# A retention decoder layer on one core: the up phase of its MLP as one written-out sequence of products

## The chip, the cores and the metric

The kernel runs on one NeuronCore of a Trainium2 chip. Five engines work side by side: TensorE (PE in the profile, its weight loads PEld) multiplies, VectorE (DVE) and GpSimd (POOL) do elementwise arithmetic, ScalarE (ACT) copies and applies functions, SyncE (SP) issues the DMAs. The metric is the device time of one execution in microseconds (us); the time of the kernel before is the median of 3 runs.

## The reference, cut to what matters

One decoder layer on 2048 positions of width 1024 in float32: a mixer of convolution and retention, cross-attention into 256 memory tokens, then a squared-ReLU MLP of hidden width 4096. After each part stands a LayerNorm of `alpha * x + f(x)`. The change touches the end of the cross-attention and the MLP.

```python
def memory_cross_attention(x, mem, w_xq, w_xk, w_xv, w_xo):
    ...
    p = jax.nn.softmax(s, axis=-1).astype(x.dtype)
    o = jnp.einsum('bhsm,bmhd->bshd', p, v).reshape(B, S, D)
    return o @ w_xo

def squared_relu_mlp(x, w_up, w_down):
    return jnp.square(jax.nn.relu(x @ w_up)) @ w_down

def reference(...):
        ...
        xa = memory_cross_attention(x, mem, w_xq[l], w_xk[l], w_xv[l], w_xo[l])
        x = layer_norm(DN_ALPHA * x + xa, ln2_g[l], ln2_b[l])
        ff = squared_relu_mlp(x, w_up[l], w_down[l])
        x = layer_norm(DN_ALPHA * x + ff, ln3_g[l], ln3_b[l])
```

## The kernel before

A float32 product is made of three passes: each operand is split into a high part (a copy by ScalarE in the type float32r, CAST in the profile) and a low part (operand minus high part), and `passes` (line 123) multiplies high by high, high by low and low by high. Both matrix products of the MLP are done as Winograd's form of Strassen's scheme: a 2 x 2 product of blocks takes seven products, numbered 1 to 7, of operands that are sums of blocks. Each product is four steps of three matmuls, 128 x 128 by 128 x 512.

**Up phase** (`up_phase`, line 958, called once for each half `h` of the positions, with 16 units `f` each). `up_weights` (886) loads the two raw tiles `ur` of the next unit, has GpSimd make four sums (`us`, `ur`, 128 x 512), and splits seven operands into tiles `uo`: copies on ScalarE, low parts on VectorE, for product 4 on GpSimd. `x_operand` (859) does the same for the position side (`er` loaded, `ehi` and `elo`), once for each half. The seven products run in the order 1, 2, 3 of the unit before, 6, 4 of the unit before, 7, 5. Products 1, 6, 5 and 3 add up in one accumulator `ua`; between them ScalarE takes a snapshot of it (`snapshot`, 943, tile `sn`), and the next product into `ua` has to wait for that. `squared` (930) adds a product and a snapshot on VectorE, applies ReLU and square on ScalarE, and stores the hidden block `hs` to DRAM. Beside this `down_weights` (898) prepares the operands of the down weights, 16 jobs spread over the phase: loads `dr`, four sums `ds` on GpSimd, seven copies and low parts `dw`, seven stores to `wdo_d`.

**Down phase** (`down_all`, line 1102, 32 steps `k`, again seven products each, at the places `u` = 0 to 6). `w_load` (1005) loads weight operands (`do`), four steps ahead, `h_load` (1016) hidden blocks (`hr`); `h_sum` (1028) makes their sums on VectorE and `h_split` (1040) the operands `ho`, with low parts on VectorE for products 6, 7 and 3 and on GpSimd for the others. `add_to` (1072) adds each product to the accumulators `acc` on VectorE. A `Norm` (1081) finishes a row of 128 positions: statistics on VectorE, the root on GpSimd, the scaling on ScalarE, gain and bias half on VectorE, half on GpSimd (`affine`, 180).

**End of cross-attention** (loop at line 1194). For each block of 128 positions scores (`psc`) and softmax, then the output product `po` (`d_out`, 786) with transposes hooked into it: `d_probs` (773, tile `dp`) of the probabilities, and `x2_turn` (806, tiles `xt`, `xv`, `xs`) of normalised rows, from which the position operands are stored to `xo_d`. The two transpose into the same few PSUM banks.

**What sets the order.** TensorE follows the program's order throughout these phases (`ordered["pe"]`). For VectorE, ScalarE and GpSimd a scheduler at compile time chooses the order, from priorities and modelled times, until `ordered["rest"]` is set, which happens in the last unit of the up phase (line 1244); after that they too follow the program. Each engine runs its instructions in the order chosen. Loads on SP keep their order among themselves. Tiles live in a fixed number of slots per tag (line 37). All instructions of PE, DVE, ACT and POOL go through the wrapper at line 60, so that the profile gives L61 for all of them and they are told apart by their tiles.

## Time and profile before

| | us |
|---|---|
| median of 3 runs (2649.84 to 2657.35) | 2650.61 |
| the profiled execution | 2645.74 |
| its span, from the first to the last instruction | 2644.0 |
| end of cross-attention, from the last scores to the first up product (1290.1 to 1324.2) | 34.1 |
| up phase (1324.2 to 1986.5) | 662.3 |
| down phase, first 50 us (1986.5 to 2036.5) | 50.0 |
| down phase, the rest, up to its last matmul (2036.5 to 2628.9) | 592.4 |
| after the last matmul | 15.1 |

All positions in the trace are us from the start of the span. An engine's busy time is the time in which one of its instructions runs; consecutive matmuls overlap, so that the distance between starts, not the duration of one, tells what a matmul costs. Idle time in front of an instruction is put down to what released it.

### The profile page before, as it was taken

Reading aid. Unit: us, or ns where it says so; the run is one execution under the profiler, and the core shown is the slowest. Engines: PE = TensorE matmul, PEld = TensorE weight load, DVE = VectorE, ACT = ScalarE, POOL = GpSimd, SP = SyncE. Lnnn points to the kernel's source line nnn. Section 1 sums busy time; section 2 is a strip of 40 time slices with the busy share of each in tenths; the row PEclk is TensorE's granted clock in tenths of the full one; section 3 lists DMA queues with packets and bytes.
Section 4 is the critical chain, followed back from the end, with each engine's and each line's share of the span. In section 5 each row is a group of like instructions: output and inputs, shape, how many; then the busy total and the mean of one; then the engine's idle time right before and its main releaser. Section 6 shows DMA issues by size and latency. Waiting matters only on the chain.

```text
span 2644.0 us, 33973 instructions
## 1 busy us (share of the span) xinstructions
PE 2546.8 (96%) x12248; PEld 2152.1 (81%) x12248; DVE 1704.2 (64%) x2675; ACT 928.7 (35%) x1667; POOL 1002.3 (38%) x908
## 2 busy tenths in 40 slices
PE   8999999998999999999889999999998999999997
PEld 7999999987889888888777877777776888778885
DVE  6888888888885644444565556555544555775557
ACT  3222322223233622222456656566552222222221
POOL 3222432215555311221255453455522322552235
PEclk9999999999999999999999999999999999999998
DMA  5222322223633502222476676677769776787774
GB/s 171 64 61 74 121 80 70 76 92 129 207 121 120 183 25 96 76 69 87 147 246 247 246 251 214 222 267 262 252 222 386 253 257 238 265 317 257 247 250 155
DMA packets 246632, 471.09 MB, mean 178 GB/s; under 512 B 19392, under 2 KB 136640, under 8 KB 246464
## 3 DMA queue, kind: packets, MB, share of 16 engines
q1 hardware_dynamic: 237104, 460.37, 50.1%
q10 hardware_dynamic: 9360, 8.56, 1.1%
q8 instruction: 96, 1.57, 0.2%
q14 instruction: 72, 0.59, 0.1%
HBM read 328.34 MB, written 140.51 MB: 177 GB/s over the span
## 4 chain that ended last, share of the span: by engine, by line
PE 78%; DVE 6%; DMA 5%; POOL 5%; ACT 3%; issue 2%; SPq 0%; POOLq 0%; ACTq 0%; DVEq 0%
PE po L61 12%; PE da L61 11%; PE ua L61 10%; PE pj L61 9%; PE pjh L61 8%; PE psc L61 7%; PE dc L61 5%; PE uc L61 4%; PE pc L61 3%; PE db L61 2%; PE ub L61 2%; DMA do<-wdo_d 2%; POOL us L61 1%; POOL ds L61 1%; PE psY L61 1%
## 5 line engine op out<-in xcount | busy, mean ns | idle before, releaser
L61 PE MATMUL da<-do,ho 128*128 128x512 f32 x1536 | 368.7, 396 | 19.2 <-DVE acc L61 12.9
L61 PE MATMUL ua<-ehi,uo 128*128 128x512 f32 x1024 | 337.7, 400 | 27.3 <-ACT sn L61 25.1
L61 PEld LDWEIGHTS da<-do,ho 128*128 128x128 f32 x1536 | 292.8, 191 | 85.1 <-DVE acc L61 14.8
L61 DVE SCALAR_TENSOR_TENSOR cacc<-u,convw,cacc 128x512 f32<-128x512 f32 x480 | 353.9, 749 | 6.8
L61 PEld LDWEIGHTS ua<-ehi,uo 128*128 128x128 f32 x1024 | 195.8, 191 | 77.3 <-ACT sn L61 30.4
L61 POOL TENSOR_TENSOR ho<-hr,ho 128x512 fp32r<-128x512 f32 x96 | 131.6, 1380 | 207.5 <-ACT ho L61 159.8
L61 PE MATMUL ua<-elo,uo 128*128 128x512 f32 x512 | 203.7, 398 | 0.0
L61 PE MATMUL pjh<-whi,xhi 128*128 128x384 f32 x512 | 186.6, 365 | 0.0
L61 POOL TENSOR_TENSOR wlo<-wraw,whi 128x384 fp32r<-128x384 f32 x128 | 127.7, 1024 | 142.2 <-ACT whi L61 129.9
L61 PE MATMUL dc<-do,ho 128*128 128x512 f32 x768 | 180.4, 390 | 1.0 <-DMA do<-wdo_d 1.0
L61 PE MATMUL pjh<-whi,xlo 128*128 128x384 f32 x512 | 172.6, 337 | 0.0
L61 PE MATMUL pjh<-wlo,xhi 128*128 128x384 f32 x512 | 172.6, 337 | 0.0
L61 PEld LDWEIGHTS dc<-do,ho 128*128 128x128 f32 x768 | 143.9, 188 | 32.3 <-DMA do<-wdo_d 2.6
L61 PE MATMUL uc<-ehi,uo 128*128 128x512 f32 x512 | 165.4, 393 | 2.5 <-DVE hs L61 2.5
L61 ACT CAST ho<-hr 128x512 fp32r<-128x512 f32 x128 | 77.3, 618 | 252.1 <-DMA hr<-h_d 90.0
L61 PE MATMUL pj<-xhi,whi 128*128 128x512 f32 x384 | 153.8, 400 | 8.0 <-ACT whi L61 6.7
L61 PE MATMUL pj<-xhi,wlo 128*128 128x512 f32 x384 | 150.5, 392 | 0.1
L61 PE MATMUL pj<-xlo,whi 128*128 128x512 f32 x384 | 150.3, 391 | 0.0
L61 ACT ACTIVATE hs<-hs 128x512 f32<-128x512 f32 x192 | 121.1, 631 | 51.7 <-DVE hs L61 49.0
L61 DVE TENSOR_TENSOR acc<-acc,da 128x512 f32<-128x512 f32 x104 | 70.8, 684 | 88.0 <-PE da L61 88.0
L61 DVE TENSOR_TENSOR uo<-us,uo 128x512 fp32r<-128x512 f32 x96 | 79.0, 832 | 61.0 <-ACT uo L61 61.0
L61 PEld LDWEIGHTS uc<-ehi,uo 128*128 128x128 f32 x512 | 96.6, 189 | 24.5 <-DVE hs L61 2.9
(212 smaller groups left out, 6037.2 us busy)
## 6 DMA issues: line engine op xcount, KB each, us to landing
do<-wdo_d SPq DMA_DIRECT2D x245, 512.0 KB, 6.4
wdo_d<-dw SPq DMA_DIRECT2D x112, 512.0 KB, 2.7
ur<-in_w_up_dram SPq DMA_DIRECT2D x64, 512.0 KB, 5.2
h_d<-hs SPq DMA_DIRECT2D x128, 256.0 KB, 3.4
hr<-h_d SPq DMA_DIRECT2D x104, 256.0 KB, 3.2
wraw<-in_w_in_dram SPq DMA_DIRECT2D x64, 384.0 KB, 3.1
dr<-in_w_down_dram SPq DMA_DIRECT2D x32, 512.0 KB, 3.8
er<-xo_d SPq DMA_DIRECT2D x28, 512.0 KB, 4.8
```

Source lines behind the costliest of these rows:

```text
L61: ins = fn(*args, **kw)
```

## The change

The two calls of `up_phase` become one function, `up_all`, over 32 units with seven steps `n` each. The products keep their sequence. A list `stream` of all weight operands is walked beside it: in each step `up_make` prepares the operand that is needed eight steps later (four and six steps in the first two units). The sums and all low parts are made by VectorE. `late` holds a low part back until the next operand is begun. ReLU and square of a block come one step after its addition. `ordered["rest"]` is set in the last block of the cross-attention, so that from there on all engines follow the program.

What happens at the borders is put down by step number (`put`): the position operands of the first half are split during the last two output products and the first steps, those of the second half in steps 106 to 118; the jobs for the down weights (`dw_load`, `dw_make`) begin about every 11.4 steps and take eight; the weight operands of the first down products are loaded from step 210 on, the first hidden block from step 215.

In the down phase all low parts of `h_split` move to VectorE; the hidden block of the next step is loaded at place 2 of a step and used from place 5 on; a norm's scaling, gain and bias become two VectorE operations of 128 x 1024 (`scalar_tensor_tensor`), and the norms get other places. The last two norms of the cross-attention use the same form. Several tiles get other tags.

Removed functions, which stand above, are left out of the diff here.

```diff
-        return layer_norm(xr, l2g, l2b, x2_d[tt * P:(tt + 1) * P, :])
+        if tt < NT - 2:
+            return layer_norm(xr, l2g, l2b, x2_d[tt * P:(tt + 1) * P, :])
...
+    waiting = []
+    def late(fn):
+        flush()
+        waiting.append(fn)
+    def flush():
+        while waiting:
+            waiting.pop(0)()
...
+    def x_split(h, i, k):
+        raw = raws.pop((h, i, k))
+        hi = sb(XTAG[i], [P, 2, 512], "ehi", F32R)
+        lo = sb(XTAG[i], [P, 2, 512], "elo", F32R)
+        act.copy(hi, raw)
+        late(lambda: lo_dve(lo, raw, hi))
+        xo.setdefault((h, i), []).append((hi, lo))
...
+    def up_load(g):
+        if g < UPS:
+            a0, a1 = sb("R", [P, D], "ur0"), sb("R", [P, D], "ur1")
+            eload(a0, a["w_up"][2 * (g % NF)])
+            eload(a1, a["w_up"][2 * (g % NF) + 1])
+            wraws[g] = [a0, a1, None]
...
+    def up_make(g, i):
+        if not 0 <= g < UPS:
+            return
+        w = wraws[g]
+        a0, a1 = w[:2]
+        if i == 6:
+            w[2] = sb("V", [P, D], "us")
+            dve.tensor_tensor(w[2][:, c0], a1[:, c0], a1[:, c1], op=ALU.add)
+            dve.tensor_tensor(w[2][:, c1], w[2][:, c0], a0[:, c0], op=ALU.subtract)
+        elif i == 7:
+            dve.tensor_tensor(a1[:, c0], a0[:, c0], a1[:, c0], op=ALU.subtract)
+        elif i == 5:
+            dve.tensor_tensor(a0[:, c1], a0[:, c1], w[2][:, c1], op=ALU.subtract)
+        src = {1: a0[:, c0], 2: a0[:, c1], 3: a0[:, c1], 4: a1[:, c1]}.get(i)
+        if src is None:
+            src = {5: w[2][:, c0], 6: w[2][:, c1], 7: a1[:, c0]}[i]
+        z = sb("B" if made[0] % 10 in (6, 7) else "Z", [P, 2, 512], "uo", F32R)
+        made[0] += 1
         act.copy(z[:, 0, :], src)
...
+        late(lambda: lo_dve(z[:, 1, :], src, z[:, 0, :]))
+        wup[g, i] = z
+        if i == 4:
+            up_load(g + 2)
...
+    def dw_load(j):
+        b0, b1 = sb("Ya", [P, D], "dr0"), sb("Ya", [P, D], "dr1")
+        eload(b0, a["w_down"][2 * j])
+        eload(b1, a["w_down"][2 * j + 1])
+        draws[j] = b0, b1, sb("W", [P, 512], "ds")
...
+    def dw_make(j, n):
+        b0, b1, t2 = draws[j]
+        i = (1, 5, 2, 6, 7, 4, 3)[n]
+        if i == 5:
+            dve.tensor_tensor(b0[:, c0], b0[:, c1], b0[:, c0], op=ALU.subtract)
+        elif i == 6:
+            dve.tensor_tensor(t2, b1[:, c1], b0[:, c0], op=ALU.subtract)
+        elif i == 7:
+            dve.tensor_tensor(b0[:, c1], b1[:, c1], b0[:, c1], op=ALU.subtract)
+        elif i == 4:
+            dve.tensor_tensor(b1[:, c0], b1[:, c0], t2, op=ALU.subtract)
...
+        z = sb(("Yb", "Yb", "V")[dn[0] % 3], [P, 2, 512], "dw", F32R)
+        dn[0] += 1
+        act.copy(z[:, 0, :], src)
+        def low():
+            lo_dve(z[:, 1, :], src, z[:, 0, :])
+            sp.dma_start(wdo_d[j][i - 1], z.bitcast(F32))
+        late(low)
...
+    def up_all(at, ahead):
+        order = [1, 2, 3, 4, 6, 7, 5]
+        stream = [(m // 7 - (order[m % 7] in (3, 4)), order[m % 7]) for m in range(7 * UPS + 7)]
+        nextop = [5]
...
+        def add(c, f, tb, ps, snap):
+            t, dst = h_tile(c, f, tb)
+            dve.tensor_tensor(t, quarters(ps), quarters(snap), op=ALU.add)
+            squares(t, dst)
...
+            if c:
+                if u == 0:
+                    c.a = pp("ua")
+                    up_product(c.a, c, 1, True)
+                    c.s1 = snapshot(c.a)
+                elif u == 1:
+                    b = pw("ub")
+                    up_product(b, c, 2, True)
+                    add(c, 0, 0, b, c.s1)
+                elif u == 3:
+                    up_product(c.a, c, 6, False)
+                    c.s2 = snapshot(c.a)
+                elif u == 5:
+                    c.c = psm("uc")
+                    up_product(c.c, c, 7, True)
+                elif u == 6:
+                    up_product(c.a, c, 5, False)
+                    c.s3 = snapshot(c.a)
+            if last:
+                if u == 0:
+                    add(last, 1, 1, last.c, last.s3)
+                elif u == 2:
+                    up_product(last.a, last, 3, False)
+                    t, dst = h_tile(last, 0, 1)
+                    act.activation(t, quarters(last.a), AF.Relu)
+                    def go(t=t, dst=dst, ps=quarters(last.a)):
+                        dve.scalar_tensor_tensor(t, ps, 0.0, t, op0=ALU.max, op1=ALU.mult)
+                        sp.dma_start(dst, t)
+                    tail.append(go)
+                elif u == 4:
+                    up_product(last.c, last, 4, False)
+                    add(last, 1, 0, last.c, last.s2)
+            for fn in before:
                 fn()
-            b = pw("ub")
-            up_product(b, c, 2, True)
-            end(2)
-            squared(c, 0, 0, b, s1)
-            if last:
-                up_rest3(last)
-            up_product(c.a, c, 6, False)
-            end(6)
-            c.s2 = snapshot(c.a)
-            if last:
-                up_rest4(last)
-            c.c = psm("uc")
-            up_product(c.c, c, 7, True)
-            end(7)
-            up_product(c.a, c, 5, False)
-            s3 = snapshot(c.a)
-            squared(c, 1, 1, c.c, s3)
-            end(5)
-            last = c
-        up_rest3(last)
-        nxt(3)
-        up_rest4(last)
-        nxt(4)
+            for fn in at.get(n, ()):
+                fn()
+            while nextop[0] < min(n + 1 + ahead(n), len(stream)):
+                up_make(*stream[nextop[0]])
+                nextop[0] += 1
...
-        tag = "X" if i in (1, 2, 6, 7) else "Ya" if i in (5, 3) or f % 4 < 2 else "V"
+        tag = "X" if i in (2, 6, 7, 5) else "Ya" if i in (3, 4) or f % 4 < 2 else "V"
...
-        (lo_dve if i in (6, 7, 3) else lo_pool)(z[:, 1], src, z[:, 0])
+        late(lambda: lo_dve(z[:, 1], src, z[:, 0]))
...
+            self.mv, self.rs = mean_rstd(self.z, D)
         def finish(self):
-            affine(self.z, l3g, l3b, self.dst)
-    NORMS = {13: [(0, 0, 3)], 14: [(0, 1, 0), (0, 2, 3)], 15: [(0, 3, 0)], 16: [(0, 4, 0), (0, 5, 3)],
-             17: [(0, 6, 0)], 18: [(0, 7, 0)],
-             29: [(1, 0, 3)], 30: [(1, 1, 0), (1, 2, 3)], 31: [(1, 3, 0), (1, 4, 3), (1, 5, 4)]}
+            z = self.z
+            dve.scalar_tensor_tensor(z, z, self.mv[:, 0:1], self.g, op0=ALU.subtract, op1=ALU.mult)
+            dve.scalar_tensor_tensor(z, z, self.rs, self.b, op0=ALU.mult, op1=ALU.add)
+            sp.dma_start(self.dst, z)
...
+    NORMS = {13: [(0, 0, 3)], 14: [(0, 1, 3)], 15: [(0, 2, 3)], 16: [(0, 3, 2)],
+             17: [(0, 4, 3)], 18: [(0, 5, 1), (0, 6, 3)], 19: [(0, 7, 2)],
+             29: [(1, 0, 3)], 30: [(1, 1, 1), (1, 2, 3)], 31: [(1, 3, 0), (1, 4, 2), (1, 5, 4)]}
...
+                todo[5].append(lambda nx=nx: (h_sum(nx, 0), h_split(nx, 1), h_sum(nx, 1), h_split(nx, 2)))
+                todo[6].append(lambda nx=nx: (h_sum(nx, 2), h_split(nx, 6), h_sum(nx, 3), h_split(nx, 7)))
+                carry.append((0, lambda nx=nx: (h_split(nx, 5), h_split(nx, 3))))
+                carry.append((1, lambda nx=nx: h_split(nx, 4)))
...
-                if u == 5 and k + 2 < DOWN:
-                    h_load(k + 2, ["Hb", "Hb", "Hb", "Ha", "Hc", "Hc", "Hc"])
+                        w_load(j, (u + 5) // 2)
+                if u == 2 and k and k + 1 < DOWN:
+                    h_load(k + 1, ["Hb", "Hb", "Hb", "Ha", "Hc", "Hc", "Hc"])
...
+            if tt == NT - 1:
+                ordered["rest"] = True
...
+                out_hooks = [(2, lambda: part(0, "R")), (5, lambda: part(1, "R")), (8, lambda: part(2, "Z")),
+                             (10, lambda: part(3, "Z")), (11, lambda: d_probs(tt, 0)),
+                             (13, lambda: d_probs(tt, 1)), (14, lambda: part(4, "V"))]
...
+            out_hooks = [(1, n14.stats), (2, lambda: part(5, "V")), (4, n14.finish), (6, lambda: up_make(0, 1)),
+                         (8, lambda: part(6, "Z")), (9, lambda: up_make(0, 2)), (11, lambda: part(7)),
+                         (13, lambda: up_make(0, 6))]
...
+    put(0, n15.stats, lambda: x2_turn(NT - 2, 0), lambda: part(8))
+    put(1, n15.finish, lambda: x2_turn(NT - 2, 1), lambda: part(9))
+    put(2, lambda: x_load(0, *parts[11], "V"), lambda: part(10))
+    put(3, lambda: up_load(1), lambda: x_load(0, *parts[12], "V"))
+    put(4, lambda: part(11), lambda: x_load(0, *parts[13], "Z"))
+    put(5, lambda: part(12))
+    put(6, lambda: part(13))
+    put(7, lambda: x2_turn(NT - 1, 0))
+    put(8, lambda: x2_turn(NT - 1, 1))
...
+    for start, end, jobs in ((14, 105, range(8)), (119, 203, range(8, 16))):
+        for m, j in enumerate(jobs):
+            n0 = start + (end - start) * m // 8
+            put(n0 - 3, lambda j=j: dw_load(j))
+            for q, o in enumerate((0, 1, 3, 4, 5, 6, 7)):
+                put(n0 + o, lambda j=j, q=q: dw_make(j, q))
+    b0 = 7 * (NF - 1)
+    for i, n in ((1, 0), (2, 1), (6, 3), (7, 5), (5, 6), (3, 9), (4, 11)):
+        for q, k in enumerate((0, 2)):
+            tag = {0: "V", 1: "Ya", 2: "Yb"}[(2 * TURN.index(i) + q) // 2 % 3]
+            put(b0 + max(n - 2, 0), lambda i=i, k=k, tag=tag: x_load(1, i, k, tag))
+            put(b0 + n + 1 + q, lambda i=i, k=k: x_split(1, i, k))
...
+    e0 = 7 * (UPS - 1)
+    put(e0 - 7, lambda: [w_load(f, 1) for f in range(DEEP)])
+    put(e0 - 2, first_hidden)
+    for n, i in ((0, 2), (1, 6), (3, 7), (5, 5)):
+        put(e0 + n, lambda i=i: [w_load(f, i) for f in range(DEEP)])
+    put(e0 + 2, sums)
+    put(e0 + 3, lambda: h_split(0, 1))
+    put(e0 + 4, lambda: h_split(0, 2), lambda: load_acc(0, 0))
+    put(e0 + 5, lambda: h_split(0, 6))
+    put(e0 + 6, lambda: h_split(0, 7))
+    put(e0 + 7, lambda: h_split(0, 5))
+    put(e0 + 9, lambda: h_split(0, 3))
+    put(e0 + 11, lambda: h_split(0, 4))
+    up_all(at, lambda n: 4 if n < 7 else 6 if n < 14 else 8)
```

## Rows read from the trace of the kernel before

**Rows 1.** The page, part 1: busy time, share of the span, instructions of TensorE.
```profile
PE 2546.8 (96%) x12248; PEld 2152.1 (81%) x12248; DVE 1704.2 (64%) x2675; ACT 928.7 (35%) x1667; POOL 1002.3 (38%) x908
```
**Rows 2.** Stages: start:end length, busy (instructions) of PE PEld DVE ACT POOL, clock, DMA share, GB/s.
```profile
1290.10:1324.20 34.10, 25.28 (x113) 20.57 (x112) 25.37 (x34) 16.67 (x22) 5.70 (x6) 0.85 0.71 225
1324.20:1986.50 662.30, 632.51 (x2706) 511.87 (x2705) 375.56 (x456) 387.07 (x675) 326.19 (x229) 0.99 0.70 244
1986.50:2036.50 50.00, 42.44 (x156) 31.42 (x156) 22.98 (x29) 10.57 (x18) 11.94 (x10) 0.90 1.02 397
2036.50:2628.90 592.40, 579.76 (x2535) 477.98 (x2533) 375.31 (x485) 134.06 (x217) 218.83 (x187) 0.99 0.72 255
2628.90:2644.00 15.10, 0.11 (x1) 0.00 (x0) 7.58 (x13) 1.89 (x2) 7.69 (x10) 0.60 0.27 104
```
**Rows 3.** Two stretches without a wait, TensorE alone: busy (instructions), clock, DMA.
```profile
1440.00:1560.00 120.00, 120.00 (x523) 1.00 0.66 233
2060.00:2260.00 200.00, 200.00 (x884) 1.00 0.72 251
```
**Rows 4.** TensorE's waits in four stages: in total, times, longest us.
```profile
PE dp L61 <- DVE xv L61: 8.8, 1, 8.8
...
PE ua L61 <- ACT sn L61: 25.1, 11, 4.2
PE uc L61 <- DVE hs L61: 2.5, 1, 2.5
PE ua L61 <- ACT uo L61: 2.1, 1, 2.1
...
PE da L61 <- DVE acc L61: 12.6, 5, 4.1
```
**Rows 5.** One stretch of low clock, TensorE alone: busy (instructions), clock, DMA.
```profile
1341.70:1345.10 3.40, 2.92 (x7) 0.50 0.78 277
```
**Rows 6.** Timeline from 1560 to 1567: start, us, instruction, [idle before <- releaser].
```profile
1560.38 1.74 POOL L61 TENSOR_TENSOR ds<-dr 128x512 f32<-128x512 f32 x1
...
1563.49 0.62 ACT L61 CAST dw<-ds 128x512 fp32r<-128x512 f32 x1 [4.08 <-POOL ds L61]
...
1565.75 0.58 ACT L61 COPY sn<-ua 128x512 f32<-128x512 f32 x1
1566.38 0.50 PE L61 MATMUL ua<-ehi,uo 128*128 128x512 f32 x1 [3.90 <-ACT sn L61]
```
**Rows 7.** Low parts on VectorE, by tile (ns min/median/max); by group (busy, mean).
```profile
L61 DVE TENSOR_TENSOR uo<-ur,uo x96: 675/685/1790, 1288.4 to 1955.9; 128x512 fp32r<-128x512 f32 x96
...
L61 DVE TENSOR_TENSOR elo<-er,ehi x28: 1208/1226/2320, 1294.5 to 1667.7; 128x1024 fp32r<-128x1024 f32 x28
...
L61 DVE TENSOR_TENSOR dw<-ds,dw 128x512 fp32r<-128x512 f32 x48 | 44.2, 921 | 42.6 <-ACT dw L61 41.2
```
**Rows 8.** Timeline of VectorE with GpSimd idle.
```profile
2105.13 0.69 DVE L61 TENSOR_TENSOR acc<-acc,dc 128x512 f32<-128x512 f32 x1 [2.03 <-PE dc L61]
2105.73 0.69 DVE L61 TENSOR_TENSOR hr<-hr 128x512 f32<-128x512 f32 x1
```
**Rows 9.** Timeline from 2284 to 2294, in the down phase.
```profile
2285.95 1.74 POOL L61 TENSOR_TENSOR ho<-hs,ho 128x512 fp32r<-128x512 f32 x1
2286.46 1.77 DVE L61 TENSOR_TENSOR hs<-hr,hs 128x512 f32<-128x512 f32 x1
...
2292.48 2.07 PE L61 MATMUL da<-do,ho 128*128 128x512 f32 x4 [4.15 <-DVE acc L61]
```
**Rows 10.** DMA issues from 1400, from 1960 and from 2040: count, KB, median us to landing.
```profile
ur<-in_w_up_dram SPq DMA_DIRECT2D x24, 512.0 KB, 5.2
...
do<-wdo_d SPq DMA_DIRECT2D x42, 512.0 KB, 8.6
...
hr<-h_d SPq DMA_DIRECT2D x36, 256.0 KB, 2.9
```
**Rows 11.** Timeline of the tail: VectorE's add of the last product.
```profile
2634.77 0.67 DVE L61 TENSOR_TENSOR acc<-acc,da 128x512 f32<-128x512 f32 x1
```

More of the change, by code (lines that the diff above doesn't have):

```diff
@@ L1170, in down_all @@
             last = c
-        for _, fn in carry:
-            fn()
         down_product(last, last.c, 4, False)
         add_to(last, 1, 0, last.c)
-        o = Norm(1, 7)
+        t0 = T + 7 * P
+        o = Norm(acc[1, 7], l3[0], l3[1], out[t0:t0 + P, :])
         o.stats()
@@ L1183, in down_all @@
         t0 = T + 6 * P
-        layer_norm_last(z, l3g, l3b, out[t0:t0 + P, :], half_stats(z, st, 1))
+        layer_norm_last(z, l3[0], l3[1], out[t0:t0 + P, :], half_stats(z, st, 1))
     for tt in range(3):
@@ L1213, in hybrid_layer, with part @@
             if tt == NT - 1:
-                up_weights(0)
-                for i in TURN[:4]:
-                    x_operand(0, i)
-                out_hooks = [(11, lambda: d_probs(tt, 0)), (13, lambda: d_probs(tt, 1))]
+                up_load(0)
+                parts = [(i, k) for i in TURN for k in (0, 2)]
+                for n in range(4):
+                    x_load(0, *parts[n], ETAG[n])
+                def part(n, more=None):
+                    x_split(0, *parts[n])
+                    if more:
+                        x_load(0, *parts[n + 4], more)
@@ L1232, in first_hidden @@
         for n in range(4):
             last_sum.append(h_sum(0, n))
-    def first_down(i):
-        if i == 7:
-            load_acc(0, 0)
-        for f in range(DEEP):
-            if i not in (3, 4):
-                w_load(f, i)
-        for j in {2: (1,), 6: (2, 6), 7: (7,), 5: (5,)}.get(i, ()):
-            h_split(0, j)
-        if i == 5:
-            ordered["rest"] = True
-    up_phase(1, {NF - 1: [first_hidden]}, first_down)
-    for i in (3, 4):
-        h_split(0, i)
+    e0 = 7 * (UPS - 1)
```

175 lines of the change are left out of this document (63 added, 112 removed).

## The prediction

> **What bounds the kernel now.** I read the totals first, then the stages, then what TensorE waited for in each, then one wait of each kind in the timeline. TensorE works through 96% of the span [rows 1], so only its lost time can be won. The table of stages [rows 2] splits the part that the change touches: the end of cross-attention (34.1 us), the up phase (662.3), the first 50 us of the down phase, the rest of it (592.4) and what follows the last product (15.1). What the work itself needs comes from two stretches without a wait [rows 3]: 120 us hold 521 up matmuls (523 less the two cut by the edges), 0.2303 us each, and 200 us hold 882 down matmuls, 0.2267 us each. The same shape is slower in the up phase; nothing in the trace says why, so both stay. A phase has 32 units x 7 products x 12 matmuls = 2688. Then:
>
> - end of cross-attention: 96 matmuls x 0.2267 + 16 transposes (0.6 us per four) = 24.2; lost 9.9
> - up: 2688 x 0.2303 + 16 transposes (2.4) = 621.4; lost 40.9
> - first 50 us of down: 154 x 0.2267 = 35.0; lost 15.0
> - rest of down: 2534 x 0.2267 = 574.4; lost 18.0
>
> The waits [rows 4] name most of it: one of 8.8 us in front of the transposes `dp`, 29.7 in the up phase (25.1 of them for the snapshot `sn` on ScalarE), 12.6 in the rest of down for `acc` on VectorE. [...]
>
> Why does ScalarE snapshot late, being busy 387 of 662 us [rows 2]? In the timeline [rows 6] it stands 4.08 us in front of `dw<-ds`, whose source GpSimd is still subtracting (1.74 us for one sum), and the snapshot is queued behind that and four more copies; TensorE waits 3.90. VectorE in the down phase shows the same [rows 9]: operands of later products at 1.77 us apiece stand in front of the add that frees `da`; TensorE waits 4.15.
>
> **The change, part by part.**
>
> 1. *Sums and low parts to VectorE.* In the up phase GpSimd issues 229 instructions [rows 2]; by the code 224 are the moved sums and low parts (4 + 1 per unit, 4 per down job). VectorE then has 456 + 224 = 680. What one costs: `uo` has minimum 675, median 685, maximum 1790 ns [rows 7]: two modes, and the slow one lies in the timeline beside a two-input GpSimd operation [rows 9]. With GpSimd idle I take the fast mode; back to back they start 0.60 us apart [rows 8]. 680 x 0.60 + 28 wide ones x 0.56 more = 424 us of some 630: 67%. In the eight steps of a down job it is (8 x 15/7 + 11) x 0.60 = 16.9 of 22.1 us. Nothing on the path. If the slow mode had another cause, a rival below has the price.
>
> 2. *The order.* The sequence of products is the same in both kernels (1, 2, old 3, 6, old 4, 7, 5); new is that ScalarE and VectorE get theirs by place. A snapshot now stands at the head of its step, and its accumulator is written again two products later: 24 x 0.2303 = 5.5 us of slack. Weights are made eight products (22 us) ahead, and the low part one make later than its copy, so VectorE never stands waiting for a copy just issued. Of the 40.9 us lost in up I leave 8.5: 1.0 where product 3 of the last unit directly follows product 5 on one accumulator, as now; 3 for the seam between the halves, where x operands add a 1024-wide copy and low part per step (bounds: 0, and 6.4 as now); 4.5 for the first unit, below. Gain 32.4.
>
> 3. *End of cross-attention and first unit.* The wait of 8.8 us ended with `xv` on VectorE: weight and x operand work stood in front of it. Now VectorE comes to `xv` before that, so the stage takes 24.2 us. Gain 9.9. But VectorE's list is long there. From 1303.4 (end of the last but one output product) I add: statistics 1.5, the norm's two new 1024-wide operations 2.4, four wide low parts at 1.16, five 512-wide ones, another norm's statistics 1.5, two sums: 14.2 us, to 1318. Then it waits for product 2 (end 1320.6) and does add 0.6, norm 2.4, two wide low parts, a sum and the low part of weight 7: done at 1327.2. Product 7 is due at 1323.9 and can run 0.45 us without it: 2.8 us of wait, and a clock stretch behind it, 1.7. The 1024-wide operation with a scalar is in no row; I take 1.2, near the free `elo` (1226 ns), the bounds being 1.2 and its maximum 2.32 [rows 7]: up to 4.5 us more. Below, 0.
>
> 4. *Start of down.* From the end of unit 31's first product to the fourth product of k = 1 lie 18 products, 49 us. In it must land 29 weight tiles, four accumulators, a hidden block and the last stores: about 20 MB. The row of that stretch moved 397 GB/s with all engines full [rows 2]: 50 us. Nearly even, so I keep 5 of the 15.0 us (bounds 0 and 15). Gain 10. [...]
>
> 5. *Rest of down.* The norms leave ScalarE and GpSimd, so VectorE's slow mode goes there too. What is late next: after product 7 VectorE does an add, two sums and the low part of the next operand 1: 0.2 + 3 x 0.60 + 0.69 = 2.7 us, wanted at 2.72 + 0.45 = 3.17. It just fits, at cost 0; with a norm's end in front it may not, and I leave 2 of the 18.0. At 0.92 apiece (the mean of `dw<-ds` [rows 7]) for the last three it would be 3.6, 0.5 late in each of 31 steps: 15 us, the upper bound. The hidden block is now loaded at place 2 for use at place 5, 8.2 us, against 2.9 to land [rows 10]. Gain 16.
>
> 6. *Tail.* VectorE's last add starts at 2634.77 [rows 11], behind a norm that went over GpSimd and ScalarE. Now, from 2626.1: 0.2 + add 0.6, statistics 1.5, half statistics 0.6, norm 2.4 after 0.3 for the root: 2631.7. Gain 3.
>
> Sum: 32.4 + 9.9 + 10 + 16 + 3 = 71.3 us. The profiled execution took 2645.74 us (span 2644.0), 4.9 under the median 2650.61; the gain is taken off the median: 2579, said as 2580.
>
> **The rivals.**
>
> *The seams keep their price.* First unit 9, seam of the halves 6.4, start of down 15, some of the norms: 30 us more, 2609. For it: my lists for these places are the least sure, and DMA is full there. Against: each wait there was for an engine out of order, and loads are pulled ahead by 7 steps. Chance 0.14.
>
> *VectorE stays slow without GpSimd,* 0.92 us each, the mean of `dw<-ds` [rows 7], instead of 0.60. A down job comes every 11.4 steps (31.4 us), with 35.4 operations: 32.6 us, 1.2 late for each of 16 jobs, 19 us less the slack of 5.5; with the 15 of point 5 that is 28 us more, 2608. Against: the two modes. Chance 0.10.
>
> *The order was no cause:* the same waits stand at other places, and 30 us of up stay: 2610. Against: rows 6 shows a queue in which the urgent copy stands last. Chance 0.05.
>
> *Slower: a load late at the head of a queue.* ScalarE's copy of the next unit's first weight waits for a load that is asked for only after a low part one step later; it is wanted 11 - 2.8 = 8.3 us after that. Lateness blocks the snapshots behind it, and TensorE loses what passes the 5.5 us of slack. So it begins to cost at a landing of 13.8 us and eats the gain at 13.8 + 71/31 = 16.1; at 17 us it gives 31 x 3.2 = 99 us, 2680. The median landing of `ur` is 5.2, and 8.6 with the DMA engines full [rows 10]. Chance 0.06, half of it near 16 us, where it ends within the measurement. [...]
>
> **How the numbers follow.** The forecast has 0.65, around 2580: 2565 if nothing of points 2 to 5 is left, 2555 if in addition the up matmuls ran at 0.2267. With the seams and the slow VectorE the range is 2563 to 2617; outside lie the late load and the far ends. Measurements of this kernel tell 0.3% (8 us) from no change: faster 0.94, same 0.03, slower 0.03.
>
> **What would show it.** TensorE's wait for `sn` gone, and the up phase 630 us long, beginning ten us earlier; VectorE's `uo` with a maximum near 700 ns, GpSimd nearly idle; one wait at product 7 of the first unit; waits for `acc` under 2 us in all; up matmuls still at 0.230 us. It is wrong if ScalarE waits for `ur` or `er` in many units, or if TensorE waits for `ho` once in each k.

## The result, and the profile after

The kernel after takes 2575.86 us (median of 4 runs, 2574.07 to 2578.04), against 2650.9 for the kernel before beside it: a ratio of 0.971, 95% interval 0.970 to 0.973. The forecast was 2580, with 2563 to 2617 as its range. The profiled execution took 2576.22 us, its span 2574.4.

The page, part 1, the line that answers to [rows 1]:

```profile
PE 2531.4 (98%) x12248; PEld 2144.9 (83%) x12248; DVE 1785.3 (69%) x3027; ACT 907.7 (35%) x1650; POOL 447.7 (17%) x505
```

The stages, as in [rows 2]: start:end length, then busy time (instructions) of PE, PEld, DVE, ACT and POOL, granted clock, DMA share, GB/s. They are again the end of cross-attention, the up phase, the first 50 us of the down phase, the rest of it, and what follows the last product:

```profile
1293.50:1317.20 23.70, 23.69 (x113) 19.38 (x112) 19.33 (x27) 12.40 (x18) 3.84 (x3) 1.00 0.93 316
1317.20:1942.20 625.00, 621.40 (x2706) 507.71 (x2706) 448.97 (x693) 391.45 (x683) 2.04 (x3) 1.00 0.76 262
1942.20:1992.20 50.00, 45.57 (x187) 35.34 (x186) 24.88 (x40) 9.34 (x16) 0.00 (x0) 0.97 1.02 393
1992.20:2562.80 570.60, 569.86 (x2505) 469.14 (x2503) 389.58 (x603) 117.44 (x203) 10.79 (x30) 1.00 0.75 262
2562.80:2574.40 11.60, 0.20 (x1) 0.00 (x0) 6.26 (x10) 0.65 (x1) 3.69 (x6) 0.61 0.24 90
```

Two stretches without a wait, as in [rows 3], TensorE alone: 0.230 us a matmul in the up phase and 0.227 in the down phase, as before (the counts are less two for the edges).

```profile
1400.00:1520.00 120.00, 120.00 (x524) 1.00 0.74 261
2020.00:2220.00 200.00, 199.99 (x883) 1.00 0.73 249
```

With these the stages can be set beside the prediction. "Lost" is the length less what the matmuls and transposes need, worked out as there. The two down stretches hold 187 + 2505 matmuls by the rows, 4 more than the 2688 there are, since those cut by an edge count twice; taking off 1.7 and 2.3, the need is 185.3 x 0.2267 = 42.0 of the first 50 us, and 2502.7 x 0.2267 = 567.4 of the other 570.6.

| | lost before | left, as predicted | left, as measured | gain predicted | gain measured |
|---|---|---|---|---|---|
| end of cross-attention | 9.9 | 0 | -0.5 | 9.9 | 10.4 |
| up phase | 40.9 | 8.5 | 3.6 | 32.4 | 37.3 |
| first 50 us of down | 15.0 | 5 | 8.0 | 10 | 7.0 |
| rest of down | 18.0 | 2 | 3.2 | 16 | 14.8 |
| after the last product (length) | 15.1 | 12.1 | 11.6 | 3 | 3.5 |
| all before the first of these | | | | 0 | -3.4 |
| sum | | | | 71.3 | 69.6 |

69.6 is the difference of the two spans, 2644.0 - 2574.4; the medians are 75.0 apart, since the profiled execution of before lies 5 us under its median. The last line but one is no part of the change: the code up to there is the same, and the first up matmul starts between 1313.9 and 1319.4 in variants of the kernel after that differ only behind it. So stages are compared by their lengths, never by positions.

TensorE's waits, as in [rows 4] (in total, times, longest, us), first in the up phase and then in the down phase:

```profile
PE uc L61 <- ACT uo L61: 2.7, 1, 2.7
PE ua L61 <- ACT sn L61: 0.7, 1, 0.7
PE ua L61 <- DVE uo L61: 0.2, 1, 0.2
...
PE da L61 <- DVE ho L61: 2.8, 3, 2.1
PE da L61 <- ACT ho L61: 1.3, 1, 1.3
PE dc L61 <- DMA do<-wdo_d: 0.9, 3, 0.3
```

Of the 25.1 us for the snapshot `sn` 0.7 are left, and the 8.8 for `xv` and the 12.6 for `acc` are gone. What is left is mostly in two places: product 7 of the first unit, and the operands of k = 2 in the down phase (1.3 and 2.1 us). VectorE's low parts, as in [rows 7], have lost their slow mode, but for one:

```profile
L61 DVE TENSOR_TENSOR uo<-ur,uo x160: 675/684/694, 1315.1 to 1928.0; 128x512 fp32r<-128x512 f32 x160
...
L61 DVE TENSOR_TENSOR uo<-us,uo x64: 679/684/1414, 1320.5 to 1923.0; 128x512 fp32r<-128x512 f32 x64
```

The one of 1414 ns starts at 1350.43, beside the only large operation that GpSimd still has in the up phase (`xv`, 1.30 us from 1349.99).

### The profile page after: what moved, and what is told of

The parts are those of the page before. It is cut to its first block, busy times and chain, and to the rows that moved or that the text cites. A ratio compares the mean times of both kernels' runs of the same rounds, so it can differ in the third digit from the quotient of the medians.

```text
span 2574.4 us, 33530 instructions
## 1 busy us (share of the span) xinstructions
PE 2531.4 (98%) x12248; PEld 2144.9 (83%) x12248; DVE 1785.3 (69%) x3027; ACT 907.7 (35%) x1650; POOL 447.7 (17%) x505
## 4 chain that ended last, share of the span: by engine, by line
PE 89%; DVE 5%; DMA 3%; ACT 1%; POOL 1%; issue 1%; SPq 0%; POOLq 0%; DVEq 0%; ACTq 0%
PE ua L61 13%; PE da L61 13%; PE po L61 11%; PE pj L61 10%; PE pjh L61 8%; PE psc L61 7%; PE uc L61 7%; PE dc L61 6%; PE db L61 3%; PE ub L61 3%; PE pc L61 3%; PE psY L61 1%; DVE yr L61 1%; DVE cacc L61 1%; DMA xraw<-in_xT_dram 1%
## 5 line engine op out<-in xcount | busy, mean ns | idle before, releaser
L61 PE MATMUL da<-do,ho 128*128 128x512 f32 x1536 | 363.5, 391 | 4.2 <-DVE ho L61 2.8
L61 PE MATMUL ua<-ehi,uo 128*128 128x512 f32 x1024 | 329.3, 392 | 0.9 <-ACT sn L61 0.7
L61 POOL TENSOR_TENSOR rs<-mv,eps_t 128x1 f32<-128x1 f32 x64 | 13.2, 206 | 1453.2 <-DVE mv L61 1453.1
L61 PEld LDWEIGHTS dc<-do,ho 128*128 128x128 f32 x768 | 143.8, 188 | 32.4 <-DMA do<-wdo_d 2.7
L61 DVE TENSOR_TENSOR uo<-ur,uo 128x512 fp32r<-128x512 f32 x160 | 108.6, 684 | 12.2 <-ACT uo L61 11.9
```

The costliest lines, as they stand in the source:

```text
L61: ins = fn(*args, **kw)
```

## The experiments

The theory was that of the prediction: the fixed order takes the waits for the snapshot away, the work that goes to VectorE costs nothing, and small waits stay at the borders. The rival was that the work's leaving GpSimd is itself the cause, and the order nothing.

### Order or engine

**Fixed order, sums back on GpSimd.**

```diff
-            dve.tensor_tensor(w[2][:, c0], a1[:, c0], a1[:, c1], op=ALU.add)
+            pool.tensor_tensor(w[2][:, c0], a1[:, c0], a1[:, c1], op=ALU.add)
...
-        late(lambda: lo_dve(z[:, 1, :], src, z[:, 0, :]))
+        late(lambda: (lo_pool if i == 4 else lo_dve)(z[:, 1, :], src, z[:, 0, :]))
```
(all four sums of a unit and of a down job)

> The changed kernel with the eight kinds of sums of the up and down weights and the low part of product 4 back on GpSimd, everything in the same fixed order. If the order is what removed the waits (theory A), ScalarE may now stand 3 to 3.5 us for two GpSimd sums in a step, which the 5.5 us of slack of a snapshot still cover: up phase 625 to 635 us, time 2576 to 2587, TensorE's wait for sn under 5 us. If the engine is what removed them (rival B), VectorE's low parts go back to the two modes (mean 0.83 to 0.93 us) and the up phase to about 650: 2600 or more.

2578.6 us, ratio 0.972 (0.970 to 0.973); the up phase takes 626.6 us from its first matmul to its last (624.6 in the kernel after; this measure is used for all the kernels below). The 2 us lie at the first unit, where the wait at product 7 is 4.4 instead of 2.7 us and the granted clock 0.50 behind it for 6.8 us. So the order alone, with the new layout, is enough.

**New layout, sums on VectorE, order of ScalarE, VectorE and GpSimd left to the scheduler** from the first up step to step 223.

```diff
-    put(e0 + 6, lambda: h_split(0, 7))
+    put(e0 + 6, lambda: h_split(0, 7), lambda: ordered.update(rest=True))
...
+    ordered["rest"] = False
     up_all(at, lambda n: 4 if n < 7 else 6 if n < 14 else 8)
```

> The changed kernel with the order of ScalarE, VectorE and GpSimd left to the scheduler from the first up step to step 223; sums and low parts stay on VectorE, the borders stay as they are. Theory A: ScalarE's queue again has copies that wait in front of snapshots, up phase 640 to 655, time 2592 to 2607, TensorE's wait for sn 15 to 25 us. Rival B: up phase below 632, time under 2584, since nothing waits for GpSimd any more.

2577.87 us, ratio 0.972 (0.970 to 0.973); up phase 625.2 us, 2.0 us of waits for the snapshot in all. So the engine alone, in the new layout, is enough too, and the theory that the order is the cause has fallen in this form.

**Both undone.** The two diffs above together.

> Both undone at once: sums and the low part of product 4 on GpSimd, and the order of the up phase left to the scheduler; borders and down phase as changed. Both theories: the up phase is near the 662 us of before less its first unit and last border, 645 to 660, time 2597 to 2612. If it is no worse than the worse of the two single ones, the two parts remove the same waits; if it is their sum, they remove different ones.

2640.24 us, ratio 0.995 (0.993 to 0.996); up phase 689.3 us: far above the 2597 to 2612 expected, and more than what either part had been thought to be worth. TensorE's waits in the up phase from 1340 to 1930:

```profile
PE ua L61 <- ACT sn L61: 45.6, 29, 3.8
```

One of them in the timeline of this kernel (start, us, instruction, [idle before <- releaser]):

```profile
1677.49 1.59 POOL L61 TENSOR_TENSOR dr<-dr 128x512 f32<-128x512 f32 x1 [1.28 <-PE ub L61]
...
1679.12 1.14 ACT L61 CAST dw<-dr 128x512 fp32r<-128x512 f32 x2 [5.36 <-POOL dr L61]
1680.16 0.58 ACT L61 COPY sn<-ua 128x512 f32<-128x512 f32 x1
...
1680.79 0.80 PE L61 MATMUL ua<-ehi,uo 128*128 128x512 f32 x1 [3.80 <-ACT sn L61]
```

This is the pattern of [rows 6] again: ScalarE stands 5.36 us for GpSimd's sum, the snapshot is queued behind two copies, TensorE waits 3.80. Beside it the kernel with the fixed order and the sums on GpSimd, its longest wait of ScalarE for a GpSimd sum, and then TensorE from 1342 to 1930 (busy, clock, DMA share, GB/s):

```profile
1627.46 0.58 ACT L61 COPY sn<-ua 128x512 f32<-128x512 f32 x1
...
1631.95 1.30 POOL L61 TENSOR_TENSOR us<-us,ur 128x512 f32<-128x512 f32 x1
...
1633.29 0.62 ACT L61 CAST uo<-us 128x512 fp32r<-128x512 f32 x1 [4.30 <-POOL us L61]
```
```profile
1342.00:1930.00 588.00, 588.00 (x2567) 1.00 0.75 260
```

ScalarE stands 4.30 us here, but the snapshot of the step went ahead of the wait. In that stretch its waits for `us` alone come to 70.7 us in 23 places, none longer than 4.3, and TensorE does not wait once. So either part breaks the chain "late sum, copy in front of the snapshot, snapshot, TensorE": the engine makes the sum early, the order takes the snapshot out from behind it.

**The kernel before with the engine changed alone** (its own order and layout).

```diff
-        ops = left_sums(a0[:, c0], a0[:, c1], a1[:, c0], a1[:, c1], sa[:, c0], sa[:, c1], sc, pool)
+        ops = left_sums(a0[:, c0], a0[:, c1], a1[:, c0], a1[:, c1], sa[:, c0], sa[:, c1], sc, dve)
...
-            split(z, ops[i], lo_pool if i == 4 else lo_dve)
+            split(z, ops[i], lo_dve)
...
-        pool.tensor_tensor(sa[:, c0], b0[:, c1], b0[:, c0], op=ALU.subtract)
+        dve.tensor_tensor(sa[:, c0], b0[:, c1], b0[:, c0], op=ALU.subtract)
```
(and the other three sums of a down job)

> The kernel before with one part of the change alone: the sums of the up phase, the low part of product 4's weight and the sums of the down weights go from GpSimd to VectorE; the order of the engines stays that of before. It is the other side of the run with the free order (the engine changed, the order free, but the new sequence of steps), and tells whether the engine alone is enough in the old kernel too. Theory A (either part alone removes the same waits): the 25 us of waits for the snapshot in the up phase go nearly all, up phase 630 to 640 us, 2620 to 2632. Rival B (the engine is enough only in the new sequence, with its loads and makes laid out by place): waits for the snapshot of 15 us or more stay, up phase 648 to 665, 2637 to 2655.

2623.07 us, ratio 0.990 (0.988 to 0.992). TensorE's waits from 1310 on:

```profile
PE da L61 <- DVE acc L61: 17.5, 7, 4.2
PE dp L61 <- DVE xv L61: 9.0, 1, 9.0
PE ua L61 <- ACT sn L61: 4.1, 3, 3.0
PE uc L61 <- DVE hs L61: 3.9, 1, 3.9
```

The waits for the snapshot fall from 25.1 to 4.1 us and the up phase from 661.9 to 634.2. So six lines that name another engine bring 28 us, over a third of the change; `xv` and `acc` stay, and they are the borders' and the down phase's.

### What a late snapshot costs

**36 dummy copies on ScalarE** right before the first snapshot of every second unit (15 times). With 12 copies instead of 36 it is the second run here.

```diff
+                    if g % 2 and g < UPS - 1:
+                        for _ in range(36):
+                            act.copy(mask, mask)
                     c.s1 = snapshot(c.a)
```

> ScalarE is given 36 dummy copies of a 128x128 tile (about 0.27 us each, 9.7 us) right before the first snapshot of every second unit, 15 times. It measures the slack of a snapshot, said in the prediction to be 5.5 us from the end of its product to the next write to its accumulator; the snapshot's own copy takes 0.62 of it, and ScalarE idles some 1 us in front of it without the dummies. Theory A (5.5 us): TensorE waits 9.7 - 1 - 4.9 = about 4 us in each of the 15 units and gets a low-clock stretch behind each (up to 1.7): 55 to 85 us more, 2630 to 2665. Rival B (no slack, all of it is lost): 15 x 9 + 25 = 160 us more, about 2735. Rival C (the accumulators are written later than that, or the copies are hidden whole): 2576 to 2585.

2706.68 us, ratio 1.020 (1.019 to 1.022). The second of the 15 places:

```profile
1391.94 11.85 ACT L61 COPY mask<-mask 128x128 f32<-128x128 f32 x36
1403.69 0.58 ACT L61 COPY sn<-ua 128x512 f32<-128x512 f32 x1
...
1404.33 0.79 PE L61 MATMUL ua<-ehi,uo 128*128 128x512 f32 x1 [5.82 <-ACT sn L61]
```

The copies took 0.33 us apiece, not 0.27: 11.75 us of delay, of which 1.0 lay before the product's end (about 1392.9). The forecast slack of 5.5 us, less 0.6 for the snapshot's own copy, leaves 11.75 - 1.0 - 4.9 = 5.9 us of wait; measured 5.82. The total lies 42 us above the range of theory A, for two reasons. The dummies were longer: the 15 waits make 92 us instead of 60 (13 of 5.1 to 6.1 us, one of 8.6, and 10.0 at the first unit so treated, where it falls to a weight copy). And the stretches of low clock are longer than the 3.4 us of [rows 5]: at 12 of the 15 places the granted clock is 0.50 for 6.8 or 10.2 us, and of the 129.7 us by which the up phase is longer than in the kernel after, 38 are no wait, 2.5 a place instead of at most 1.7.

> ScalarE is given 12 dummy copies of a 128x128 tile right before the first snapshot of every second unit, 15 times; with 36 of them (11.8 us, as measured) TensorE waited 5.7 us per unit. Theory A (a snapshot has 4.9 us of slack once its own copy is taken off, and all that passes it is lost): 12 x 0.33 = 3.9 us of ScalarE stay under it, no wait for a snapshot, 2574 to 2582. Rival B (what is lost is a share of about one half of any delay): 15 x 1.9 = 29 us more plus clock stretches, 2600 to 2620.

2579.92 us, ratio 0.973 (0.972 to 0.975); no wait for a snapshot but the 0.7 us at the end of the phase, as without dummies. For a snapshot 3.9 us of delay were free and 11.8 cost what passed the slack (5.82): no share of the delay was lost, only the excess. The delay was not free everywhere: at the first unit so treated, where weights are made only four to six steps ahead, TensorE waits 2.1 us for a weight copy (0.2 us for its low part there in the kernel after).

**A unit's raw weights asked for right before its first copy.**

```diff
+        if i == 1 and g > 1:
+            up_load(g)
...
-        if i == 4:
-            up_load(g + 2)
```

> The raw weights of a unit are asked for right before the copy that needs them, in the same step, instead of some eleven steps ahead; ScalarE then stands for the whole landing of the load once in each of 30 units. The prediction's price for that: TensorE loses only what passes the 5.5 us between the end of a snapshot's product and the next write to its accumulator. Theory A (slack as predicted): a landing of 4.2 us with the DMA engines half idle (median of the up phase's loads) plus the issue, about 5 us of standing, costs nothing or nearly so; 2576 to 2590, up phase 625 to 639. Rival B (no slack: what blocks the head of ScalarE's queue blocks TensorE): 30 x (5 - 1) = 120 us more and low-clock stretches behind each, 2695 to 2745.

2579.1 us, ratio 0.972 (0.971 to 0.974). The edit did less than meant: SP does not hold the load until the copy (in the longest case it issues it at 1573.32, 6.70 us ahead of the copy), and ScalarE stood for it in only 6 units between 1400 and 1900, 23.8 us in all. The longest:

```profile
1573.32 1.40 SPq L104 DMA_DIRECT2D ur<-in_w_up_dram  x2
...
1580.02 0.62 ACT L61 CAST uo<-ur 128x512 fp32r<-128x512 f32 x1 [7.31 <-DMA ur<-in_w_up_dram]
1580.55 0.58 ACT L61 COPY sn<-ua 128x512 f32<-128x512 f32 x1
...
1581.18 0.50 PE L61 MATMUL ua<-ehi,uo 128*128 128x512 f32 x1 [1.70 <-ACT sn L61]
```

7.31 us at the head of ScalarE's queue cost TensorE 1.70, the only wait for a snapshot but the 0.7 us at the end of the phase. That is the mechanism of the rival "late load", at the price that the slack gives; the rival's 30 units were not reached. The 4.2 us that the expectation takes for a landing are the median of the kernel after from 1400 to 1700, where the DMA engines were not half idle: their share was 0.76.

### Holding the low parts back

```diff
     def late(fn):
-        flush()
-        waiting.append(fn)
+        fn()
```

> The low part of every operand of the up and down phases stands right behind its copy in VectorE's list, instead of one make later. Theory A (the holding back is what keeps VectorE from standing at the head of its queue): VectorE now stands 0.6 us and more for ScalarE's copy in front of about 400 low parts, up to 240 us of idle more, mostly covered by its third of free time in the up phase, but not in the down phase, where two sums and two low parts of the next operand have 3.17 us: 31 steps x about 0.6 to 1.2 us = 19 to 37 us more there; 2590 to 2620. Rival B (VectorE has room enough, the holding back is worth nothing): 2573 to 2581.

2577.08 us, ratio 0.971 (0.969 to 0.973). VectorE now stands 66.3 us in front of `uo` from 1400 to 1900, against 18.1 in the kernel after, and the snapshots lose 3.5 us in all against 0.7. In the down phase nothing came of the expected 19 to 37 us: from 1992 on TensorE has no wait of a hidden operand at all. The expectation had overlooked that without holding back the low part of operand 1 stands in front of the second sum instead of behind it, 0.6 us earlier. So holding back is worth at most some 3 us (those of the snapshots; the ratio is that of the kernel after), and not needed in the down phase.

### The down phase's low parts and norms

```diff
-        late(lambda: lo_dve(z[:, 1], src, z[:, 0]))
+        late(lambda: (lo_dve if i in (6, 7, 3) else lo_pool)(z[:, 1], src, z[:, 0]))
...
-                o = Norm(acc[h, tt], l3[0], l3[1], out[t0:t0 + P, :])
+                o = OldNorm(acc[h, tt], l3[0], l3[1], out[t0:t0 + P, :])
```
(`OldNorm` scales on ScalarE and puts gain and bias half on GpSimd, as before)

> The changed kernel with the down phase's low parts for products 1, 2, 5 and 4 on GpSimd and its norms scaled by ScalarE and finished half by VectorE, half by GpSimd, at the new places. My point 5 says the waits for acc came from VectorE operations of 1.8 us beside GpSimd: the rest of the down phase goes from 571 to 580 to 590 us, time 2586 to 2596, waits for acc 8 to 15 us. The rival says the places of the norms alone removed them: 571 to 575, time under 2580.

2593.11 us, ratio 0.977 (0.976 to 0.979), 17 us more than the kernel after. TensorE's waits:

```profile
PE da L61 <- POOL ho L61: 14.8, 8, 3.5
PE da L61 <- DVE acc L61: 3.1, 2, 1.9
```

The price is that of the prediction's point 5; the place is another. In the fixed order TensorE waits for GpSimd's low part itself, not for the add on VectorE that a slow low part delays. The waits for `acc` did not come back as expected: 4.8 us with one of 1.7 for `dc`, against 8 to 15. For them the rival is right, the norms' new places are enough; its time under 2580 is not. The run moves low parts and norms at once, and only its trace tells them apart: seven of the eight waits for `ho` come in steps with a norm, as at 2213.25, where GpSimd does gain and bias of a norm (1.80 and 1.62 us) right before the two low parts that TensorE needs. From 1990 on, no step without a norm has one. What the low parts on GpSimd would cost without the norms, no run shows.

### The borders, and a faster version

**The last norm's end moved from step 1 of the up phase to step 4.** The wait that is left there, in the timeline of the kernel after:

```profile
1324.34 1.28 DVE L61 SCALAR_TENSOR_TENSOR xd<-xd,mv,bc_ln_g 128x1024 f32<-128x1024 f32 x1
1325.73 1.28 DVE L61 SCALAR_TENSOR_TENSOR xd<-xd,rs,bc_ln_b 128x1024 f32<-128x1024 f32 x1
1326.93 1.22 DVE L61 TENSOR_TENSOR elo<-er,ehi 128x1024 fp32r<-128x1024 f32 x1
1328.07 0.68 DVE L61 TENSOR_TENSOR ur<-ur,ur 128x512 f32<-128x512 f32 x1
...
1328.84 0.62 ACT L61 CAST uo<-ur 128x512 fp32r<-128x512 f32 x1 [3.21 <-DVE ur L61]
...
1329.51 0.55 PE L61 MATMUL uc<-ehi,uo 128*128 128x512 f32 x1 [2.66 <-ACT uo L61]
```

```diff
-    put(1, n15.finish, lambda: x2_turn(NT - 2, 1), lambda: part(9))
+    put(1, lambda: x2_turn(NT - 2, 1), lambda: part(9))
...
-    put(4, lambda: part(11), lambda: x_load(0, *parts[13], "Z"))
+    put(4, n15.finish, lambda: part(11), lambda: x_load(0, *parts[13], "Z"))
```

> The last norm's two 1024-wide operations go from step 1 of the up phase to step 4. Theory A (the 2.66 us wait in front of product 7 of the first unit comes from VectorE's list, in which these 2.6 us stand ahead of the sum that ScalarE waits for): the wait goes, and with it the low-clock stretch behind it (up to 1.7 us): 2 to 5 us less, 2571 to 2574. Rival B (something else would be late there, x operands or the first weight's landing): a wait of over 1.5 us stays at products 6 to 5 of the first unit, 2575 to 2577. Rival C (the norm's later end delays the transposed rows or the sums of unit 1): a new wait of 2 us or more in units 1 or 2.

2571.72 us, ratio 0.970 (0.968 to 0.971). The wait is gone, and the low-clock stretch behind it; three waits of 0.16 to 0.39 us for low parts take its place. The trace is surer than the 4.1 us between the medians, since the runs of the two kernels overlap (2570.81 to 2575.97, and 2574.07 to 2578.04).

**Besides, the down phase's low parts not held back from k = 2 on.**

```diff
         late(lambda: lo_dve(z[:, 1], src, z[:, 0]))
+        if k > 1:
+            flush()
```

> Two edits to the kernel after: the last norm's end at step 4 of the up phase (as in the run before, 2571.7), and the low parts of the down phase's hidden operands right after their copies from the third k on. In the run without any holding back the two waits of 0.34 us at the norms of the down phase were gone. Theory A (the low part of the next operand 1 is ready 0.6 us earlier, since it no longer stands behind the second sum): these two waits go, 0.7 us less, 2570 to 2572. Rival B (VectorE stands for ScalarE's copies, and the adds that free the accumulators come late): waits for the accumulators or hidden operands of 0.3 us or more in most of 29 steps, 2580 to 2592.

2569.54 us, ratio 0.970 (0.968 to 0.971). The two waits of 0.34 us are gone. Besides, the wait of 2.1 us for an operand of k = 2 is 1.4, and the stretch of low clock behind it is gone too, which the expectation had not named.

**Besides, the hidden block of k = 2 asked for two products earlier.** In the kernel after its four loads are issued from 1969.00 on, with all DMA engines full (share 1.03 from 1965 to 1979); ScalarE and then VectorE wait for them:

```profile
1969.00 3.80 SPq L104 DMA_DIRECT2D hr<-h_d  x4
...
1978.28 0.62 ACT L61 CAST ho<-hr 128x512 fp32r<-128x512 f32 x1 [17.90 <-DMA hr<-h_d]
...
1979.72 0.69 DVE L61 TENSOR_TENSOR hs<-hr 128x512 f32<-128x512 f32 x1 [4.05 <-DMA hr<-h_d]
```

```diff
+                if u == 0 and k == 1:
+                    h_load(2, ["Hb", "Hb", "Hb", "Ha", "Hc", "Hc", "Hc"])
...
-                if u == 2 and k and k + 1 < DOWN:
+                if u == 2 and k > 1 and k + 1 < DOWN:
```

> As the last one, and the second half's block of hidden rows for k = 2 is asked for two products earlier (right after the first product of k = 1, ahead of the weights asked for there). Theory A (the 3.4 us of waits for this block in the first 50 us of the down phase are its late issue): they go, and 3 us or less come out, 2567 to 2570. Rival B (the DMA engines are full there, and what the block gains the weights behind it lose): the same 3 to 4 us are lost in front of weight tiles, 2570 to 2574. Rival C (its buffers are not free that early, and the queue stands): slower by 2 us or more.

2565.27 us, ratio 0.968 (0.966 to 0.969), faster than both kernels and 4.3 us less than the version without this edit, run beside it. All waits of TensorE from 1310 on, and the first 50 us of its down phase, columns as in [rows 2]:

```profile
PE dc L61 <- DMA do<-wdo_d: 1.0, 3, 0.3
PE da L61 <- DVE ho L61: 0.8, 1, 0.8
PE ua L61 <- ACT sn L61: 0.7, 1, 0.7
PE ua L61 <- DVE uo L61: 0.5, 2, 0.4
PE uc L61 <- DVE uo L61: 0.3, 1, 0.3
```
```profile
1937.80:1987.80 50.00, 49.05 (x213) 39.52 (x212) 26.56 (x42) 9.47 (x16) 0.00 (x0) 1.00 1.02 395
```

213 matmuls instead of 187 in the same 50 us, at the same bytes per second: (213 - 1.7) x 0.2267 = 47.9, 2.1 us lost instead of 8.0. Not all of it is this load's. The version without this edit held 196:

```profile
1939.80:1989.80 50.00, 46.08 (x196) 35.92 (x196) 25.27 (x41) 9.46 (x16) 0.00 (x0) 1.00 1.01 392
```

(196 - 1.7) x 0.2267 = 44.0, 6.0 us lost. So the place of the load is worth 3.9 us here, near the 4.3 of the medians, and the low parts not held back 2.0. The weights behind the block lost nothing: `do` still has its three waits of 0.3 us. The wait of 0.8 us for `ho` lies behind this stretch (1992.86).

## Why the prediction was right, and where its steps were not

The total is near the forecast in part because errors cancel: the up phase gained 4.9 us more than predicted, the start of the down phase 3.0 and its rest 1.2 less.

1. *Sums and low parts to VectorE at no cost.* Right. Alone in the up phase, VectorE does them in 675 to 694 ns but for one, is busy 449 of 625 us (424 predicted), and TensorE waits 0.2 us for it behind the first unit's wait. The rival "VectorE stays slow without GpSimd" is out. But the step put this part of the change down as costless and worth nothing, and that was wrong: in the old kernel it brings 28 us by itself. The reason for it stood in the prediction's own reading of [rows 6], where the first link is a GpSimd sum of 1.74 us; it was followed only to the queue (in which three more copies stood, not four).

2. *The order.* The gain was 37.3 us, 32.4 predicted, and the slack of 5.5 us holds (5.82 measured where it gives 5.9). The attribution was half wrong: the step put the gain down to the order alone, and that it came does not speak for that; order and engine remove the same waits, and what one is worth depends on whether the other is there. In the new layout the order is worth 62 us with the sums on GpSimd (2640.24 - 2578.6) and 2 us, not measurable, with them on VectorE. The rival "the order was no cause" is half right: with the sums on VectorE the order adds nothing that can be measured; but the 30 us of waits that it saw staying did not stay, since the engine removes them. Mis-sized was the seam of the halves: 0 instead of 3 us, the lower bound. The step's remark on held-back low parts is worth at most 3 us.

3. *End of cross-attention and first unit.* Right: 23.7 us (24.2), the wait for `xv` gone, and 2.66 us of wait at product 7 (2.8) with one low-clock stretch behind it (granted clock 0.50 from 1329.8 to 1333.2). The 1.7 us counted for that clock are what such a stretch lost in the kernel before: behind the wait up to 1856.94 ten up matmuls took 3.99 us, where ten times 0.2303 are 2.30; eight behind the wait at [rows 5] (4.23 us, up to 1342.18) took 3.28 us, 1.4 lost. The engine is not what removed the wait for `xv` (with the engine changed alone it is 9.0 us); that VectorE's order did is read from its list, and no run undoes it alone. The last link at product 7 was not the low part, as the list had it, but ScalarE's copy behind the sum `ur`, which stands in the same list behind the norm. That 2.66 comes so near 2.8 is partly luck: the list had two wide low parts in front of the sum, where only one stood, and left out the copy of 0.62 us. The 1024-wide operation with a scalar takes 1.28 us, near the lower bound that was taken (1.2). That the norm is the cause of this wait was shown by moving it.

4. *Start of down.* The weakest step. 8.0 us were lost instead of 5, and the reasoning failed: it took the bytes to be the limit. Three waits of 0.3 us were for weights; 3.4 us were for the hidden block of k = 2, asked for at place 2 and needed at place 5, with all DMA engines full (share 1.02). TensorE's idle time (4.4 us) and one low-clock stretch (1.7: ten matmuls from 1981.79 on take 3.96 us instead of 2.27) make 6.1 of the 8.0; the rest, matmuls a little slower than 0.2267 us, is not explained. The prediction had that load in point 5 at the landing of a quiet stretch (2.9 us [rows 10]), not at that of this one: there ScalarE's copy began 9.3 us after the issue. With the load two products earlier and the low parts not held back, 2.1 us were left at 395 GB/s, 3.9 of the gain being the load's.

5. *Rest of down.* Right in size: 3.2 us left (2), two waits of 0.34 us each after a norm, and the price of the old engines at 17 us with the gain measured at 14.8. The mechanism was right in part. The step took VectorE's slow mode beside GpSimd as what makes `acc` late; with the old engines at the new places the waits for `acc` come to 4.8 us, and 14.8 us are lost for GpSimd's own low parts, nearly all behind a norm. The list itself is seen at the first of the two norms:

```profile
2305.02 1.28 DVE L61 SCALAR_TENSOR_TENSOR acc<-acc,rs,bc_ln_b 128x1024 f32<-128x1024 f32 x1
2306.22 0.68 DVE L61 SCALAR_TENSOR_TENSOR acc<-acc,dc 128x512 f32<-128x512 f32 x1
2306.82 0.68 DVE L61 TENSOR_TENSOR hs<-hr 128x512 f32<-128x512 f32 x1
2307.54 0.69 DVE L61 TENSOR_TENSOR hs<-hs,hr 128x512 f32<-128x512 f32 x1
2308.15 0.68 DVE L61 TENSOR_TENSOR ho<-hr,ho 128x512 fp32r<-128x512 f32 x1
...
2308.88 0.97 PE L61 MATMUL da<-do,ho 128*128 128x512 f32 x3 [0.34 <-DVE ho L61]
```

   Add, two sums and a low part take 2.6 us from 2306.22 on, as worked out; they begin late because the norm's end stands ahead of them.

6. *Tail.* Right: 3.5 us (3).

Of the other rivals, "the seams keep their price" is out (30 us; all seams together lose about 12), and "a load late at the head of a queue" did not occur in the kernel after, where the median landing of `ur` in the up phase was 4.5 us; its price was shown by the dummies and by the one wait of 1.70 us. In the run with 36 dummies the snapshot began when the last of them was through, 10.8 us after its product.

Open is why the new layout with both parts undone is worse in the up phase than the old kernel (689.3 against 661.9 us): ScalarE's waits there are of the same kinds (59.6 us for GpSimd's `dr`, 56.3 for the loads of `dr`; before, 56.7 for `ds` and 49.7 for the loads), and no run separates them. Open is also why an up matmul takes 0.230 us and a down matmul 0.227.

## What to carry to other kernels

When a chain of waits has several links (a slow source, a copy that waits for it, an urgent copy queued behind), two parts of a change may each break it, and their worth does not add up: ask of each part what it is worth if the other is there. The lateness of an urgent operation cost here only what passed its slack (nothing of 3.9 us, 5.82 of 11.75), which can be counted in products from the listing; standing of 4.3 us or less was free, in 23 places of one run. Count the slack of every operation in the queue behind, and at the start of a phase by itself: there 3.9 us of delay cost 2.1. At a border between phases, take the landing time of that place for each load, not that of the quiet phase (9.3 us from issue to copy here, against 2.9).

## What the hardware showed beyond that

- Full DMA engines did not mean that TensorE had to wait: at 392 and 395 GB/s (DMA share 1.01 and 1.02) the 50 us held 196 and 213 matmuls, by nothing but the place of one load in the queue.
- Not every wait is followed by a stretch of granted clock 0.50, and the length of the wait does not settle it. In the kernel before, one of 2.07 us (up to 1856.94) had a stretch of 3.4 us behind it and one of 2.50 us (up to 1363.83) none. Two waits of 1.33 and 1.35 us, 2.1 us apart, had none with the down phase's low parts alone not held back; two of 1.34 and 1.37, 2.1 us apart, had one of 3.4 us with no low part held back at all. Nor are the prediction's 1.7 us behind a wait an upper bound: two waits of 1.35 and 2.08 us (the late load, from 1980.8 on) had 6.8 us at 0.50. From the first up matmul on, the fastest version shows none before its last product.
- With GpSimd at the sums in the fixed order, VectorE's low part of `us` has a median of 1112 ns (maximum 1778) against 684, and a GpSimd sum into `us` 1624 ns; TensorE paid nothing for it from 1342 to 1930.
